# 7-product pairs of a hybrid decoder trunk: the block of the fourth sum's second half and its weights moved by 64 bytes, and four raw weight buffers for five

## The chip, the core and the metric

The kernel runs on one core of one Trainium2 chip. Its engines are TensorE (PE, whose weight loads the profile shows as PEld), VectorE (DVE), ScalarE (ACT), GpSimd (POOL) and SyncE (SP); each works through its own list of instructions, and semaphores order them among each other. The metric is the device time of one execution in microseconds.

## The reference, cut to what matters

Two layers work on x of 512 tokens and 1024 channels in float32. Each has a mixer sub-layer (four token mixers, gates and an output projection) and a gated feed-forward sub-layer. The change lies in the latter:

```python
hf = rms_norm(x, norm_ffn_pre[l])
u = causal_depthwise_conv(hf @ ffn_w_up[l], ffn_conv_w[l], ffn_conv_b[l])
gate, val = jnp.split(u, 2, axis=-1)
f = (jax.nn.gelu(gate, approximate=True) * val) @ ffn_w_down[l]
x = x + rms_norm(f, norm_ffn_post[l])
```

`ffn_w_up[l]` is 1024 x 5632: 22 blocks of 128 gate columns and 22 of value columns.

## The kernel before

**Arithmetic.** Each float32 operand is held as the sum of a high and a low part that PE takes (`hi`, `lo`). A product is three matmuls with 128x128 weights: high weights with the high and with the low activations, and low weights with the high activations. A weight unit comes by DMA from `wts` into a raw tile of 128x1024 (one of `NRAW` = 5, in `w_dma`), and is then split: ACT copies the high part into a tile `whi`, DVE subtracts to get `wlo`. There are four such pairs of tiles (`NSPL`). Each has 128 columns to spare, and `place` puts the units of the 7-product pairs (key `"fs"`) 16 columns, 64 bytes, further on in them.

**The up projection.** A pair i is one gate block and the value block that belongs to it. Pairs 0 and 1 run in the head of the stage (tile `hd`, 256-column matmuls), pairs 2 to 4 and 21 with 512-column matmuls (tile `ps`), and pairs 5 to 20 (`SEVEN`) with seven products of half size in place of eight: the 2x2 block form of a matrix product (two halves of the channels by two halves of the tokens) with sums of activations and sums of weights. In `seven(i)` a product is a call of `product(bank, weights, column, operand, first)`: 12 matmuls of 256 columns, for four blocks of 128 channels (kt) the triple high-high, high weights with low activations, low weights with high activations. Three PSUM banks, `sa`, `sb` and `se`, collect them. ACT copies (`ca`, `cb`) and DVE additions combine the parts, and `ffn_pair` makes from them the convolution, the gate and the product (`fu`).

A 7-product pair takes four weight units: 0 is the gate block from `wts`, 1 is sums of weights from a DRAM tensor that GpSimd's accumulating DMAs have made before, 2 is a half of such sums beside a half from `wts` (two DMAs into one raw tile), and 3 is a half more, which goes into a small slot (`rs`), not into a raw tile. Unit 2 is `w2`: its columns 0 to 511 meet the sum of activations `d3`, its columns 512 to 1023 the sum `d4`. The last two products of a pair (`four` and `three`) run between the first products of the next.

**The sums of activations.** `forms(h)` makes `d1` to `d4` on DVE before the 7-product pairs begin, for the first half of the four kt (h = 0) and for the second (h = 1). Each is then split by `hilo` into two of the `NG` = 60 small slots of 128x512: ACT the high part (`t1h` ... `t4h`), DVE the low part (`t1l` ... `t4l`). `side` hands the slices to `product`.

**Order.** SP and GpSimd run what the code emits, in that order; a raw tile's load is emitted in `w_dma` as soon as fewer than `NRAW` raw tiles are in use, and it waits on the chip until DVE has finished with the tile's former content. In the up projection PE too runs in the order of the code. ACT's and DVE's lists come from a scheduler that goes by the dependencies and its own estimates.

Of the kernel before, what the change touches and what calls it, by code (L numbers as in the profile page):

```python
# [10 lines left out]
F32R = mybir.dt.float32r  # L11
AF = mybir.ActivationFunctionType
ALU = mybir.AluOpType
# [19 lines left out]

WMAX = 1024

def place(k):


    return 16 if k[0] == "fs" else 0
# [12 lines left out]
NCST = 2120  # L52


NG = 60
NRAW = 5
NSPL = 4

MANUAL = {mybir.EngineType.SP, mybir.EngineType.Pool}
# [55 lines left out]
def build(tc, x, wts, prm, gains, cst, out, order=None):  # L115
# [3 lines left out]
    order = [] if recording else order  # L119
    V, A, G, T, SP = nc.vector, nc.scalar, nc.gpsimd, nc.tensor, nc.sync  # L120
    with ExitStack() as ctx:
        pool = lambda name, bufs, **k: ctx.enter_context(tc.tile_pool(name=name, bufs=bufs, **k))
        pc = pool("cst", 1)
# [8 lines left out]
        def nm(s):  # L132
            uid[0] += 1
            return f"{s}{uid[0]}"

        def slot(w=512, dt=F32, name="g"):
            return pg.tile([128, w], dt, tag="g", bufs=NG, name=nm(name))

# [6 lines left out]
        def f(t):  # L145
            return t.bitcast(F32)
# [11 lines left out]
        raw, parts = {}, {}  # L158
# [9 lines left out]
        def w_dma():  # L168
            while pos["dma"] < len(order) and sum(not isinstance(r, list) for r in raw.values()) < NRAW:
                i = pos["dma"]  # L170
# [65 lines left out]
        def split_tiles(i):  # L236
            ts = [pw.tile([128, WMAX + 128], F32R, tag=t, bufs=NSPL, name=nm(t)) for t in ("whi", "wlo")]
            return [t[:, place(order[i][1]):] for t in ts]

        def halves(i, *srcs):  # L240

            hi, lo = split_tiles(i)
            c = 0
            for s, n in srcs:
                A.activation(hi[:, c:c + n], s, AF.Copy)  # L245
                V.tensor_tensor(lo[:, c:c + n], s, f(hi[:, c:c + n]), op=ALU.subtract)  # L246
                c += n
            parts[i] = (hi, lo)

        def w_seven(i):  # L250

            r = raw.pop(i)
            halves(i, (r[0], 512) if isinstance(r, list) else (r, 1024))

        def w_split(q, roomy=False):
# [113 lines left out]
        def hilo(src, scale=1.0, name="hl"):  # L369
            dve(0.62)  # L370
            hi = slot(dt=F32R, name=name + "h")
            lo = slot(dt=F32R, name=name + "l")
            if scale == 1.0:
                A.activation(hi, src, AF.Copy)
                V.tensor_tensor(lo, src, f(hi), op=ALU.subtract)
            else:
                A.activation(hi, src, AF.Copy, scale=scale)
                V.scalar_tensor_tensor(lo, src, scale, f(hi), op0=ALU.mult, op1=ALU.subtract)
            return hi, lo
# [218 lines left out]
        pr = prm_tile()  # L598
        hT_hi = pc.tile([128, 8, 512], F32R, name="hT_hi")
        hT_lo = pc.tile([128, 8, 512], F32R, name="hT_lo")  # L600
        scr = {}
        for l in range(L):
            scr[l, 0] = pd.tile([S, D], F32, name=f"scr{l}a")
# [46 lines left out]
        for l in range(L):  # L650
# [59 lines left out]
            for kv, b in enumerate((kcb, vcb)):  # L710
                for g in range(2):
                    t = slot(name="F")
# [625 lines left out]
            for want in main_gen():  # L1338
                if isinstance(want, tuple):
                    while want[1] not in done:  # L1340
                        r = step()
# [8 lines left out]
                while (credit > 0 or behind() > MAXB) and state["alive"]:  # L1350
                    r = step()
# [45 lines left out]
            form = {n: [] for n in ("d1", "d2", "d3", "d4")}  # L1397

            def forms(h):
                def block(t, k, q):  # L1400
                    return f(t[:, k * 4 + h * 2:k * 4 + h * 2 + 2, q * 256:q * 256 + 256])
                hi, lo = (lambda k, q: block(hT_hi, k, q)), (lambda k, q: block(hT_lo, k, q))
                sub, add = ALU.subtract, ALU.add
                a, b = slot(name="ta"), slot(name="tb")
                V.tensor_tensor(v2(a), hi(0, 0), hi(0, 1), op=sub)
                V.tensor_tensor(v2(b), lo(0, 0), lo(0, 1), op=sub)
                V.tensor_tensor(a, a, b, op=add)
                form["d1"].append(hilo(a, name="t1"))
                V.scalar_tensor_tensor(v2(b), v2(a), -1.0, hi(1, 1), op0=ALU.mult, op1=sub)
                V.tensor_tensor(v2(b), v2(b), lo(1, 1), op=sub)  # L1410
                form["d2"].append(hilo(b, name="t2"))
                c = slot(name="tc")
                V.scalar_tensor_tensor(v2(c), v2(b), -1.0, hi(0, 0), op0=ALU.mult, op1=sub)
                V.tensor_tensor(v2(c), v2(c), lo(0, 0), op=sub)
                form["d3"].append(hilo(c, name="t3"))
                d = slot(name="td")
                V.scalar_tensor_tensor(v2(d), v2(b), -1.0, hi(1, 0), op0=ALU.mult, op1=sub)
                V.tensor_tensor(v2(d), v2(d), lo(1, 0), op=sub)
                form["d4"].append(hilo(d, name="t4"))

            def side(n, kt):
                if n in form:
# [4 lines left out]
            def product(b, w, c, n, first):  # L1427

                o = b[:, 0:256]
                kw = {} if first else {"skip_group_check": True}  # L1430
                for kt in range(4):
                    hi, lo = side(n, kt)
                    k = c + kt * 128
                    mm(o, wc(w[0], k), hi, first and kt == 0, False, **kw)
                    mm(o, wc(w[0], k), lo, False, False, **kw)
                    mm(o, wc(w[1], k), hi, False, kt == 3, **kw)
# [7 lines left out]
            def seven(i):  # L1444

                ba, bb, be = bank("sa"), bank("sb"), bank("se")
                sa, sb = slot(name="ca"), slot(name="cb")
                L_, R_ = slice(0, 256), slice(256, 512)  # L1450
                w0 = w_get(l, ("fs", i, 0))
                w_ahead(1)
                product(ba, w0, 0, (0, 0), True)
                A.activation(sa[:, L_], ba[:, L_], AF.Copy)
                w_ahead(2)
                more()
                product(bb, w0, 512, (1, 0), True)
                V.tensor_tensor(bb[:, L_], bb[:, L_], sa[:, L_], op=ALU.add)
                w1 = w_get(l, ("fs", i, 1))
                w_ahead(2)  # L1460
                product(ba, w1, 0, "d2", False)
                A.activation(sa[:, R_], ba[:, L_], AF.Copy)
                w_ahead()
                more()
                product(be, w1, 512, "d1", True)
                w2 = w_get(l, ("fs", i, 2))
                product(ba, w2, 0, "d3", False)
                A.activation(sb[:, L_], ba[:, L_], AF.Copy)
                w_ahead()

                def four():
                    product(ba, w2, 512, "d4", False)
                    V.tensor_tensor(ba[:, R_], be[:, L_], sb[:, L_], op=ALU.add)

                def three():
                    w3 = w_get(l, ("fs", i, 3))
                    product(be, w3, 0, (1, 1), False)
                    V.tensor_tensor(bb[:, R_], be[:, L_], sa[:, R_], op=ALU.add)
                    ffn_pair(i, [bb, ba], -1.0)
                rest.extend((four, three))  # L1480

            forms(0)
# [152 lines left out]
```

## Time and profile before

| | us |
|---|---|
| median of three runs | 1863.5 (1863.27 to 1864.52) |
| the profiled execution | 1876.15 |
| its span | 1874.3 |
| PE busy | 1851.3 (99%) |
| DVE busy | 1407.6 (75%) |
| ACT busy | 984.8 (53%) |
| granted TensorE clock, mean | 0.999 |

The profiled execution takes 12.65 us more than the median of the runs without a profile. A row of a timeline gives the start in microseconds from the span's start, the duration, the engine, the line, output and inputs by their names in the program, and in brackets the idle time before it with what ended it. A matmul's duration reaches past the start of the next, so the pace is read from start to start. "PEld" rows are the loads of weights into PE.

### The profile page before, as it was taken

To read this page: it belongs to the slowest core of one execution; us is meant where nothing else is said; L and a number is where in the kernel's file an instruction comes from. 1 tells how busy PE (TensorE), PEld (TensorE's weight loads), DVE (VectorE), ACT (ScalarE), POOL (GpSimd) and SP (SyncE) were. 2 spreads that over 40 slices of the span, in tenths; PEclk is the share of its full clock that TensorE was granted. 3 is DMA by queue.
4 is the path that set the end of the run, shared out by engine and by line. 5 is a ranking of instruction groups with operands and counts; after the bars stand their busy time and mean duration, and the time that the engine had idled before them with its cause. 6 is when DMAs were issued, how large, how long until landed. Compare 5 with 4: busy or idle time off the path is not lost.

```text
span 1874.3 us, 28621 instructions
## 1 busy us (share of the span) xinstructions
PE 1851.3 (99%) x10524; PEld 1622.7 (87%) x10524; DVE 1407.6 (75%) x2572; ACT 984.8 (53%) x1856; POOL 244.8 (13%) x397
## 2 busy tenths in 40 slices
PE   7999999999999999999999999999999999999998
PEld 7988888888788899988898888888878898999886
DVE  6898879888547888882468987897985578888732
ACT  5547576732435566662345675776224444666521
POOL 1403321100401000000023034201013010000000
PEclk9999999999999999999999999999999999999999
DMA  9524596765975356544465256958559653565332
GB/s 324 162 91 109 153 201 140 156 185 155 205 190 188 102 180 195 184 143 132 155 210 142 68 147 164 188 125 174 167 163 225 179 184 98 190 195 180 127 112 68
DMA packets 121069, 302.52 MB, mean 161 GB/s; under 512 B 16224, under 2 KB 16608, under 8 KB 120928
## 3 DMA queue, kind: packets, MB, share of 16 engines
q1 hardware_dynamic: 95328, 252.43, 42.4%
q0 software_dynamic: 25600, 48.26, 15.6%
q8 instruction: 83, 1.36, 0.3%
q14 instruction: 58, 0.48, 0.1%
HBM read 277.55 MB, written 75.50 MB: 188 GB/s over the span
## 4 chain that ended last, share of the span: by engine, by line
PE 95%; DVE 2%; issue 1%; ACT 1%; POOL 0%; DMA 0%; SPq 0%; DVEq 0%; POOLq 0%; ACTq 0%
PE ps L346 45%; PE tk L346 17%; PE sa L346 10%; PE hd L346 5%; PE se L346 5%; PE o L346 3%; PE sb L346 2%; PE vt L346 2%; PE sB L346 1%; PE sA L346 1%; PE tr L435 1%; PE tB L1128 1%; PE tA L1128 1%; PE cmp L346 0%; PE tA L1227 0%
## 5 line engine op out<-in xcount | busy, mean ns | idle before, releaser
L284 ACT ACTIVATE whi<-raw 128x1024 fp32r<-128x1024 f32 (+2 forms) x254 | 237.2, 940 | 450.8 <-PE ps L346 247.4
L285 DVE TENSOR_TENSOR wlo<-raw,whi 128x1024 fp32r<-128x1024 f32 (+2 forms) x254 | 271.0, 1072 | 211.8 <-ACT whi L284 210.2
L346 PE MATMUL ps<-hT_hi,whi 128*128 128x512 f32 x976 | 383.4, 393 | 0.9 <-DVE ob L1147 0.9
L346 PE MATMUL ps<-hT_hi,wlo 128*128 128x512 f32 x976 | 381.1, 390 | 0.0
L346 PE MATMUL ps<-hT_lo,whi 128*128 128x512 f32 x976 | 380.9, 390 | 0.0
L346 PEld LDWEIGHTS ps<-hT_hi,whi 128*128 128x128 f32 x976 | 183.4, 188 | 38.4 <-DVE ob L1147 1.7
L346 PEld LDWEIGHTS ps<-hT_hi,wlo 128*128 128x128 f32 x976 | 183.3, 188 | 38.3
L346 PEld LDWEIGHTS ps<-hT_lo,whi 128*128 128x128 f32 x976 | 183.5, 188 | 35.6
L950 DVE SCALAR_TENSOR_TENSOR acc<-ct,prm,acc 128x511 f32<-128x511 f32 (+14 forms) x240 | 175.5, 731 | 3.4
L246 DVE TENSOR_TENSOR wlo<-raw,whi 128x1024 fp32r<-128x1024 f32 x96 | 117.0, 1219 | 21.5 <-ACT whi L245 21.5
L346 PE MATMUL tk<-whi,fh 128*128 128x512 f32 x336 | 130.9, 390 | 0.0
L346 PE MATMUL tk<-whi,fl 128*128 128x512 f32 x336 | 130.8, 389 | 0.0
L346 PE MATMUL tk<-wlo,fh 128*128 128x512 f32 x336 | 130.7, 389 | 0.0
L401 POOL TENSOR_TENSOR sm<-sm,mhalf 128x1 f32<-128x1 f32 x32 | 22.1, 691 | 811.1 <-DVE sm L400 811.1
L245 ACT ACTIVATE whi<-raw 128x1024 fp32r<-128x1024 f32 x96 | 101.8, 1060 | 48.3 <-PE se L346 26.8
L1107 ACT ACTIVATE P<-P,sm 128x256 f32<-128x256 f32 (+3 forms) x128 | 70.6, 554 | 28.7 <-DVE sm L1105 28.3
L346 PEld LDWEIGHTS tk<-whi,fl 128*128 128x128 f32 x336 | 63.1, 188 | 13.2
L346 PEld LDWEIGHTS tk<-whi,fh 128*128 128x128 f32 x336 | 63.1, 188 | 13.0
L346 PEld LDWEIGHTS tk<-wlo,fh 128*128 128x128 f32 x336 | 63.1, 188 | 12.9
L346 PE MATMUL hd<-hT_hi,bh 128*128 128x256 f32 x256 | 64.5, 289 | 0.0
L346 PE MATMUL hd<-hT_hi,bl 128*128 128x256 f32 x256 | 63.6, 285 | 0.0
L214 POOL DMA_DIRECT2D sum<-wts x32 | 36.9, 1153 | 188.5 <-DMA sum<-wts 188.0
(354 smaller groups left out, 4731.0 us busy)
## 6 DMA issues: line engine op xcount, KB each, us to landing
raw<-wts SPq DMA_DIRECT2D x230, 512.0 KB, 4.2
raw<-wts SPq DMA_DIRECT2D x98, 256.0 KB, 4.3
sum<-wts SPq DMA_DIRECT2D x64, 256.0 KB, 5.0
sum<-wts SPq DMA_DIRECT2D x32, 512.0 KB, 5.8
sum<-wts POOLq DMA_DIRECT2D x64, 256.0 KB, 10.9
sum<-sum POOLq DMA_DIRECT2D x64, 256.0 KB, 11.1
raw<-sum SPq DMA_DIRECT2D x32, 512.0 KB, 4.1
br<-wts SPq DMA_DIRECT2D x40, 256.0 KB, 6.1
```

The source lines that it names most:

```text
L214: G.dma_start(s1, b(i + 1, 512), accum_op=ALU.add)
L245: A.activation(hi[:, c:c + n], s, AF.Copy)
L246: V.tensor_tensor(lo[:, c:c + n], s, f(hi[:, c:c + n]), op=ALU.subtract)
L284: A.activation(hi[:, c:c + n], s, AF.Copy)
L285: V.tensor_tensor(lo[:, c:c + n], s, f(hi[:, c:c + n]), op=ALU.subtract)
L346: T.matmul(o, lhsT=lhsT, rhs=rhs, start=start, stop=stop, **kw)
L401: G.tensor_tensor(v[:, 1:2], v[:, 0:1], mhalf[:, 0:1], op=ALU.pow)
L435: T.transpose(bs[t, h][:, k * 128:k * 128 + 128], y[h][:, k * 128:k * 128 + 128], ident)
L950: V.scalar_tensor_tensor(acc[i][:, k:], ct[i][:, :512 - k], w[:, 30 - k:31 - k], acc[i][:, k:], op0=ALU.mult, op1=ALU.add)
L1107: A.activation(P[i], P[i], AF.Exp, bias=mn[:, i:i + 1], scale=-1.0, accum_out=sm[:, i:i + 1])
L1128: T.transpose(B[j][:, (i - j) * 128:(i - j) * 128 + 128], P[i][:, j * 128:j * 128 + 128], ident)
```

## The change

Three things change.

- In unit 2 the second 512 columns lie 16 columns further on than before: the unit occupies 2 x 528 columns of its `whi` and `wlo` tile, of which 2 x 512 are written. The split writes both blocks with one ACT and one DVE instruction over a view of 128x2x512, and `four()` reads its weights from column `APART` = 528.
- For h = 1 the parts of `d4` go into a tile of their own, `t4`, at columns 16 to 527 (high) and 528 to 1039 (low), in place of two small slots. For h = 0 nothing changes.
- `NRAW` falls from 5 to 4 and `NG` from 60 to 59.

The number of instructions on each engine is the same as before. By the addresses that the built program gives the tiles, counted within 512 bytes, the activations of all sums and of `hT_hi` and `hT_lo` start at byte 416 and the weights of the 7-product units at byte 480, in both programs; in the changed one the moved weight block starts at byte 32, and the moved half of `d4` at byte 480.

```diff
+APART = 528
-NG = 60
-NRAW = 5
+NG = 59
+NRAW = 4
 ...
         def w_seven(i):
             r = raw.pop(i)
+            if order[i][1][2] == 2:
+                whole = split_tiles(i)
+                hi, lo = (t[:, :2 * APART].rearrange("p (k c) -> p k c", k=2)[:, :, :512] for t in whole)
+                v = r.rearrange("p (k c) -> p k c", k=2)
+                A.activation(hi, v, AF.Copy)
+                V.tensor_tensor(lo, v, f(hi), op=ALU.subtract)
+                parts[i] = tuple(whole)
+                return
             halves(i, (r[0], 512) if isinstance(r, list) else (r, 1024))
 ...
+        t4 = pc.tile([128, 1152], F32R, name="t4")
 ...
-                form["d4"].append(hilo(d, name="t4"))
+                if h == 0:
+                    form["d4"].append(hilo(d, name="t4"))
+                    return
+                hi_, lo_ = t4[:, 16:528], t4[:, 528:1040]
+                A.activation(hi_, d, AF.Copy)
+                V.tensor_tensor(lo_, d, f(hi_), op=ALU.subtract)
+                form["d4"].append((hi_, lo_))
 ...
                 def four():
-                    product(ba, w2, 512, "d4", False)
+                    product(ba, w2, APART, "d4", False)
```

The scheduler orders ACT and DVE anew. This is ACT in layer 0 where the 7-product pairs begin, before the change; `t3h` and `t4h` are high parts of the sums for h = 1, `fu` the first step of `ffn_pair` for pairs 3 and 4, `ca` the first copy of pair 5.

```order
L374 ACTIVATE t3h_6617<-tc_6614 128x512
L374 ACTIVATE t4h_6624<-td_6621 128x512
L1377 ACTIVATE fu_6693<-ps_6628,prm_75 128x512
L1377 ACTIVATE fu_6694<-ps_6659,prm_75 128x512
L1377 ACTIVATE fu_6765<-ps_6703,prm_75 128x512
L245 ACTIVATE whi_6806<-raw_6578 128x1024
L1377 ACTIVATE fu_6766<-ps_6734,prm_75 128x512
L1454 ACTIVATE ca_6778<-sa_6775 128x256
```

And ACT at the same place, changed:

```order
L387 ACTIVATE t3h_6616<-tc_6613 128x512
L1392 ACTIVATE fu_6687<-ps_6625,prm_75 128x512
L1392 ACTIVATE fu_6688<-ps_6656,prm_75 128x512
L1392 ACTIVATE fu_6762<-ps_6697,prm_75 128x512
L249 ACTIVATE whi_6803<-raw_6645 128x1024
L1392 ACTIVATE fu_6763<-ps_6731,prm_75 128x512
L1438 ACTIVATE t_78<-td_6620 128x512
L1475 ACTIVATE ca_6775<-sa_6772 128x256
```

The high part of the fourth sum (`t4h`, now `t`) has moved behind four `fu` and a `whi`, directly ahead of `ca`.

DVE there before the change, from the last step of the fourth sum, `td`, on:

```order
L1418 TENSOR_TENSOR td_6621<-td_6621,hT_lo 128x512
L375 TENSOR_TENSOR t4l_6625<-td_6621,t4h_6624 128x512
L1380 SCALAR_TENSOR_TENSOR fu_6693<-ps_6628,prm_75,fu_6693 128x511
L1380 SCALAR_TENSOR_TENSOR fu_6694<-ps_6659,prm_75,fu_6694 128x511
L1380 SCALAR_TENSOR_TENSOR fu_6693<-ps_6628,prm_75,fu_6693 128x510
L1380 SCALAR_TENSOR_TENSOR fu_6765<-ps_6703,prm_75,fu_6765 128x511
L1380 SCALAR_TENSOR_TENSOR fu_6694<-ps_6659,prm_75,fu_6694 128x510
L246 TENSOR_TENSOR wlo_6807<-raw_6578,whi_6806 128x1024
L1380 SCALAR_TENSOR_TENSOR fu_6765<-ps_6703,prm_75,fu_6765 128x510
L1380 SCALAR_TENSOR_TENSOR fu_6766<-ps_6734,prm_75,fu_6766 128x511
```

And changed:

```order
L1395 SCALAR_TENSOR_TENSOR fu_6687<-ps_6625,prm_75,fu_6687 128x511
L1395 SCALAR_TENSOR_TENSOR fu_6688<-ps_6656,prm_75,fu_6688 128x511
L1433 TENSOR_TENSOR td_6620<-td_6620,hT_lo 128x512
L1395 SCALAR_TENSOR_TENSOR fu_6762<-ps_6697,prm_75,fu_6762 128x511
L1395 SCALAR_TENSOR_TENSOR fu_6687<-ps_6625,prm_75,fu_6687 128x510
L1395 SCALAR_TENSOR_TENSOR fu_6688<-ps_6656,prm_75,fu_6688 128x510
L1395 SCALAR_TENSOR_TENSOR fu_6762<-ps_6697,prm_75,fu_6762 128x510
L250 TENSOR_TENSOR wlo_6804<-raw_6645,whi_6803 128x1024
L1395 SCALAR_TENSOR_TENSOR fu_6763<-ps_6731,prm_75,fu_6763 128x511
L1439 TENSOR_TENSOR t_78<-td_6620,t_78 128x512
L1479 TENSOR_TENSOR sb_6773<-sb_6773,ca_6775 128x256
```

The low part of the fourth sum (`t4l`, now `t`, L1439) has moved behind the `fu` and the first `wlo`, and the last step of `td` behind two `fu`.

## Rows read from the trace of the kernel before

**Rows 1.** The page: busy time, share and count of each engine over the span.

```profile
PE 1851.3 (99%) x10524; PEld 1622.7 (87%) x10524; DVE 1407.6 (75%) x2572; ACT 984.8 (53%) x1856; POOL 244.8 (13%) x397
```

**Rows 2.** PE's waits: engine, tile, line, releaser; total us, times, longest.

```profile
PE sa L346 <- ACT ca L1454: 0.8, 2, 0.4
```

**Rows 3.** Windows, head then 7-product: us; busy PE, PEld, DVE, ACT, POOL; PEclk, DMA, GB/s.

```profile
606.30:615.90 9.60, 9.60 (x82) 9.60 (x82) 6.49 (x8) 5.61 (x7) 0.00 (x0) 1.00 0.67 220
700.00:790.00 90.00, 90.00 (x767) 90.00 (x766) 77.35 (x111) 62.01 (x92) 0.00 (x0) 1.00 0.60 188
```

**Rows 4.** Tiles `hd`, then `sa`, weight loads: ns least/median/most, first and last start.

```profile
L346 PEld LDWEIGHTS hd<-hT_lo,bh x256: 192/192/192, 15.8 to 1544.7; 128*128 128x128 f32 x128
...
L346 PEld LDWEIGHTS sa<-t4h,whi x128: 187/192/193, 659.2 to 1737.5; 128*128 128x128 f32 x128
L346 PEld LDWEIGHTS sa<-t4l,whi x128: 187/188/192, 659.4 to 1737.6; 128*128 128x128 f32 x128
```

**Rows 5.** PE's timeline: start, us, engine, line, operation [idle before, releaser].

```profile
640.22 0.39 PE L346 MATMUL ps<-hT_lo,whi 128*128 128x512 f32 x1
...
642.03 0.39 PE L346 MATMUL ps<-hT_hi,whi 128*128 128x512 f32 x1
...
652.90 0.28 PE L346 MATMUL sb<-hT_hi,wlo 128*128 128x256 f32 x1
653.58 0.39 PE L346 MATMUL sa<-t2h,whi 128*128 128x256 f32 x1 [0.40 <-ACT ca L1454]
653.81 0.29 PE L346 MATMUL sa<-t2l,whi 128*128 128x256 f32 x1
```

**Rows 6.** ACT's timeline at the start of layer 0's 7-product stretch.

```profile
649.01 0.63 ACT L374 ACTIVATE t4h<-td 128x512 fp32r<-128x512 f32 x1 [2.70 <-DVE td L1418]
649.55 2.10 ACT L1377 ACTIVATE fu<-ps,prm 128x512 f32<-128x512 f32 x3
651.53 1.06 ACT L245 ACTIVATE whi<-raw 128x1024 fp32r<-128x1024 f32 x1
652.48 0.78 ACT L1377 ACTIVATE fu<-ps,prm 128x512 f32<-128x512 f32 x1
653.14 0.39 ACT L1454 ACTIVATE ca<-sa 128x256 f32<-128x256 f32 x1
```

**Rows 7.** DVE's timeline there.

```profile
649.67 0.69 DVE L375 TENSOR_TENSOR t4l<-td,t4h 128x512 fp32r<-128x512 f32 x1 [0.70 <-ACT t4h L374]
650.34 3.39 DVE L1380 SCALAR_TENSOR_TENSOR fu<-ps,prm,fu 128x511 f32<-128x511 f32 x5
```

**Rows 8.** SP's DMA issues in the steady 7-product stretch.

```profile
742.37 0.33 SPq L182 DMA_DIRECT2D raw<-sum  x1
...
744.20 0.43 SPq L185 DMA_DIRECT2D raw<-wts  x1
746.63 0.33 SPq L188 DMA_DIRECT2D raw<-wts  x1
752.26 0.33 SPq L182 DMA_DIRECT2D raw<-sum  x1
```

**Rows 9.** ACT's timeline there: splits of the raw tiles loaded by Rows 8.

```profile
754.17 1.06 ACT L245 ACTIVATE whi<-raw 128x1024 fp32r<-128x1024 f32 x1 [0.96 <-PE se L346]
...
761.19 1.06 ACT L245 ACTIVATE whi<-raw 128x1024 fp32r<-128x1024 f32 x1 [0.35 <-PE sb L346]
```

**Rows 10.** The page, DMA issues: count, KB each, median us from issue to landing.

```profile
raw<-wts SPq DMA_DIRECT2D x230, 512.0 KB, 4.2
```

**Rows 11.** End of layer 0's mixer: DMA issues, SP's and ACT's timeline.

```profile
raw<-wts SPq DMA_DIRECT2D x3, 512.0 KB, 11.0
...
497.27 5.35 SPq L188 DMA_DIRECT2D raw<-wts  x4
...
508.95 0.63 ACT L284 ACTIVATE whi<-raw 128x512 fp32r<-128x512 f32 x1 [0.72 <-ACT th L927]
```

**Rows 12.** ACT's timeline in layer 0's down projection.

```profile
896.94 0.63 ACT L275 ACTIVATE bh<-raw 128x512 fp32r<-128x512 f32 x1 [4.83 <-DMA raw<-wts]
```

## The prediction

> **What bounds the kernel now.** I read the page first: TensorE is busy for 99% of the span [rows 1]. The reader is to see there that only two things can move the time: a change in the pace at which matmuls follow each other, or a stall of PE made or removed. Next come PE's waits: the one wait that lies in the stretch that the change touches is that of `sa` for ACT's `ca`, 0.8 us in two places, one for each layer [rows 2]. Third, the windows: in the 7-product stretch PE and the weight load are both busy for the whole 90 us, DVE for 77.35 us and ACT for 62.01 us, at a granted clock of 1.00 [rows 3]. So there a weight load of 128x128 runs under every matmul of 256 columns and never stops; where both are full, the pace is set by how soon load and matmul let each other go on.
>
> That pace differs by place. The windows count every record that touches them, and a matmul of 0.28 us touches the next two, so some 2.4 records are to be taken off: 9.60/(82-2.4) = 120.6 ns in the head's 256-column matmuls, 90.00/(767-2.4) = 117.7 ns in the 7-product stretch [rows 3]. The loads agree: 192 ns in the head's last group; in a 7-product group 192 ns for the first of each three, but 188 ns for the next [rows 4]. In the built program before, the head's weight blocks start at the same byte as its moving operand, counted within 512 bytes; those of the 7-product units lie 64 bytes further. So a distance of 64 bytes goes with about 120.6 - 117.7 = 2.9 ns less for each matmul.
>
> **Placement, part by part.** The 7-product stretches hold 32 pairs of 84 matmuls, 2,688 in all. The change moves the second block of each third weight unit, and the half of the fourth sum that it calls `t4`. Matmul counts and instruction shapes stay, so only the distance between a running matmul's moving operand and the block loaded under it changes. From the addresses of the two built programs: 160 transitions have both operands moved, distance still 64 bytes, cost 0; 30 lose it (the last matmul on `t4` against the next product's unmoved weights), 30 x 2.9 ns = +0.09 us; 222 go to 128 bytes (the two k-tiles of the fourth sum that stay in place, and the transitions into them). The trace of before has no stretch at 128 bytes. From above, 128 acts as 0 does: 222 x 2.9 = +0.6 us. From below, the load ceases to pace at all: 512-column matmuls, whose loads hide, follow each other in (642.03 - 640.22)/8 = 0.226 us [rows 5], 113 ns for 256 columns, so 222 x (113.1 - 117.7) = -1.0 us. I take 0, the value at 64 bytes, the nearest row in distance. The rest of the 2,688 stay as they are.
>
> The Trainium skill, "SBUF — State Buffer", section "Who interferes with whom", states that PE reads SBUF through two independent ports, one for the moving operand and one for the weight load, and that PE never waits on anyone. By that rule no address could matter, the placement term would be 0 and the sum 1862.15 instead of the 1862.2 below. The 188 and 192 ns [rows 4] speak against it, though weakly, since head and 7-product groups differ in more than addresses.
>
> **The split in one operation over two blocks.** ACT and DVE each write 2x512 instead of 1024 elements, 32 times each. The nearest rows: on ACT 0.95 us from start to start for 1,024 elements (651.53 to 652.48) and 0.54 us for 512 (649.01 to 649.55) [rows 6]. Were the two halves paid as two instructions, that would be 0.13 us more for each pair, on an engine with idle time in every pair. Below nothing there is no reason for a gain. Taken at 0 either way for the end: ACT has 28 us idle in 90, DVE 12.65 [rows 3].
>
> **ACT's order at the start of the 7-product stretch.** This is the largest term. PE's matmul of 652.90 is followed by one at 653.58 instead of 653.02, and the next comes 0.23 us later instead of 0.12 [rows 5]: 0.56 + 0.11 = 0.67 us lost, in layer 1 likewise (the second of the two waits [rows 2]); together 1.34 us. What PE waits for is ACT: `t4h` sits 2.70 us on DVE's `td` until 649.01, and three `fu`, a `whi`, a `fu` and then `ca` queue behind it, so `ca` starts at 653.14 and ends at 653.53 [rows 6]. In the changed order that activation stands behind these five, directly ahead of `ca`. The three `fu` then run in what was ACT's wait for `td` (their sums are finished by 645 us, since a 24-matmul chain of 226 ns takes 5.4 us and the last one ends at about 650.2). The `whi` needs the split tile that this last chain frees, so it starts at about 650.2; 650.2 + 0.95 + 0.66 + 0.54 gives `ca` a start at about 652.35 and an end at 652.74. PE would be due at 653.02. So the stall goes whole, with 0.28 us to spare less the signal from ACT to PE (0.05 us in before, 653.53 to 653.58): -0.67 us x 2 = -1.34 us. Bounds: 0 if another wait puts `ca` back by 0.8 us or more, and not more than -1.34, because behind it PE is at its pace. What is late next: DVE computes the low part of `t4` at 649.67, after 0.70 us of waiting; in the new order seven `fu` of 0.66 us and a `wlo` of some 1.1 us go ahead of it, and the wait is gone: 649.67 - 0.70 + 5.8 = 654.8 [rows 7]. The first load for the fourth product starts at 659.2 [rows 4], and six matmuls on its first half take 0.7 us more before that part is read. 4.4 us remain.
>
> **Four raw buffers.** Each load now waits for one release more, so it is issued when the load behind it was. In the steady 7-product stretch SP issues one pair's three loads at 742.37, 744.20 and 746.63, and the next pair's first at 752.26 [rows 8]; the splits that read the first and the third start at 754.17 and 761.19 [rows 9]. A load takes 4.2 us [rows 10]. Shifted by one, these two land at 748.4 and 756.5: 5.8 and 4.7 us ahead of their splits. Cost 0; the cover is those 4.7 us. At the end of the mixer it is thinner: four loads are issued from 497.27 on, some 1.7 us apart, and take 11.0 us at the median, so the first lands by about 508.3 for a split at 508.95 [rows 11]. Shifted by 1.7 us it would come about 1 us late for ACT; PE, which has no wait for a load or a split in its list, reads such a tile later still. In the down projection ACT already waits for a load, 4.83 us at 896.94 [rows 12], and PE, which reads those tiles only in the next stage, has no wait of that kind. I take 0 for all three, with up to +1 us for the range from the mixer's end. The 60th small slot is given up together with two slots that the fourth sum no longer takes, so nothing waits longer for a slot in the stretch.
>
> **Sum.** Against the profiled execution: span 1874.3 + 0.09 - 1.34 = 1873.0, execution 1876.15 - 1.25 = 1874.9. The runs' median, 1863.5, lies 12.65 us (0.7%) below that execution; a term of 1.25 us is the same in both: 1863.5 - 1.25 = 1862.2 us.
>
> **Rivals.**
> - The stall stays, or another takes its place: `ca` still comes late since the `fu` or the `whi` ahead of it wait for something that the row does not show. For it: in before ACT ran those five back to back, so their own waits are hidden. Against: their producers' rows end by 650.2. Time: 1863.5 + 0.09 = 1863.6.
> - The distance of 128 bytes has a price of its own: 1862.8 if it acts as 0 does, 1861.2 if loads are freed. Nothing in the trace speaks for either.
> - The change does not do what it says: a 64-byte step has no effect on any transition, and the 2.9 ns of the head come from something else. Then -1.34 alone: 1862.15. The skill's rule on ports above is this case.
> - Slower: four buffers starve the splits of the 7-product stretch. It decides where a load takes more than 4.2 + 4.7 = 8.9 us. Were they as slow as at the mixer's end, 11.0 us [rows 11], each pair's third split would be 2.1 us late, and if PE had no distance to it, 32 x 2.1 = +67 us: 1929. Against it: 4.2 us there, in a stretch whose DMA share is 0.60 [rows 3].
>
> **How the numbers follow.** Forecast 0.51 (1862.2). No address effect at all 0.10 (1862.15). Stall stays 0.19 (1863.6). A price of 128 bytes 0.12 (1861.2 to 1862.8). Starved splits, in full or in part, 0.05, ending above 1867.2. On the fast side 0.03 is left for what no row shows: 3.7 us over the 222 transitions would be 17 ns each, three times the bound. About 0.2%, or 3.7 us, is what a measurement of this kernel can tell from no change; every case but the last two lies within it: faster 0.03, same 0.92, slower 0.05. The range: low 1863.5 - 1.34 - 1.04 = 1861.1, less 0.2 for the runs' own lower spread, 1860.9; high 1863.6 + 0.6 + 1.0 for late loads = 1865.2. These leave out some 0.1 to 0.15.
>
> **What would show it.** Right: no gap of 0.68 us ahead of the first `sa<-t2h` of each layer, the wait of `sa` for `ca` gone from PE's list, the pace there 117.7 ns still, load times of 188 and 192 in the fourth product as elsewhere. Wrong: a new entry in PE's waits on `whi` or `wlo` or on raw loads, ACT waiting for a load in the 7-product stretch, a pace of the fourth product under 115 or at 120 ns, or a span that moved by more than 3 us.

## The result: 15 us slower, of which the first profiles show 4.5

| | us |
|---|---|
| before, median (4 runs beside the changed kernel) | 1863.38 (1863.12 to 1864.52) |
| changed, median of 4 runs | 1878.62 (1877.27 to 1880.66) |
| ratio, with its 95% interval | 1.0081 (1.0064 to 1.0099) |
| changed, profiled execution and its span | 1880.66, 1878.9 |
| before, the execution behind the rows above, and its span | 1876.15, 1874.3 |

The forecast was 1862.2 us, within 0.2% of before. The profiled execution of the changed kernel is one of its four runs, the longest; that of before lies 12.65 us over the median of its own. So the two profiles differ by 4.5 us where the runs differ by 15.2, and whoever compares the two traces alone looks for the wrong thing.

What the prediction looked at first went as it said. Changed kernel, the page's busy times:

```profile
PE 1852.7 (99%) x10524; PEld 1624.5 (86%) x10524; DVE 1408.0 (75%) x2572; ACT 986.8 (53%) x1856; POOL 244.0 (13%) x397
```

PE is busy for 99% as in [rows 1], 1.4 us more in all, and that tells nothing of what follows. PE's waits (engine, tile, line, releaser; total us, times, longest):

```profile
PE sA L359 <- DVE mix L945: 1.5, 2, 0.8
PE ps L359 <- DVE ob L1162: 1.4, 2, 0.7
PE sC L359 <- DVE pcTl L388: 1.0, 2, 0.5
PE sB L359 <- DVE sm L1120: 1.0, 2, 0.5
```

The wait of `sa` for `ca` [rows 2] is gone; the waits of `sA` and `sB` are new, that of `ps` for `ob` and of `sC` are longer than in the kernel before:

```profile
PE ps L346 <- DVE ob L1147: 0.9, 2, 0.4
PE sC L346 <- DVE pcTl L375: 0.7, 2, 0.4
```

ACT's timeline at the start of layer 0's 7-product stretch in the changed kernel, to be read beside [rows 6]:

```profile
648.38 2.10 ACT L1392 ACTIVATE fu<-ps,prm 128x512 f32<-128x512 f32 x3
652.34 1.06 ACT L249 ACTIVATE whi<-raw 128x1024 fp32r<-128x1024 f32 x1 [1.85 <-PE ps L359]
653.30 0.76 ACT L1392 ACTIVATE fu<-ps,prm 128x512 f32<-128x512 f32 x1
653.97 0.62 ACT L1438 ACTIVATE t<-td 128x512 fp32r<-128x512 f32 x1
654.48 0.37 ACT L1475 ACTIVATE ca<-sa 128x256 f32<-128x256 f32 x1
```

The stretch begins at 652.36 here, so `ca` starts 2.12 us into it (the working had 2.16) and PE goes on without a gap, where [rows 5] had 0.68 us. PE's timeline, changed kernel:

```profile
655.07 0.28 PE L359 MATMUL sb<-hT_hi,wlo 128*128 128x256 f32 x1
655.19 0.28 PE L359 MATMUL sa<-t2h,whi 128*128 128x256 f32 x1
```

That gap was more than a loss: in most executions of the kernel before, PE goes over to a faster pace behind it, as the following runs show.

### The profile page after: what moved, and what is told of

Same layout as the page of the kernel before. It is cut to its first block, busy times and chain, and to the rows that moved or that the text cites. A ratio compares the mean times of both kernels' runs of the same rounds, so it can differ in the third digit from the quotient of the medians.

```text
span 1878.9 us, 28672 instructions
## 1 busy us (share of the span) xinstructions
PE 1852.7 (99%) x10524; PEld 1624.5 (86%) x10524; DVE 1408.0 (75%) x2572; ACT 986.8 (53%) x1856; POOL 244.0 (13%) x397
## 3 DMA queue, kind: packets, MB, share of 16 engines
q8 instruction: 82, 1.34, 0.3%
## 4 chain that ended last, share of the span: by engine, by line
PE 96%; DVE 2%; issue 1%; POOL 0%; ACT 0%; DMA 0%; SPq 0%; DVEq 0%; POOLq 0%; ACTq 0%
PE ps L359 45%; PE tk L359 17%; PE sa L359 10%; PE hd L359 5%; PE se L359 5%; PE o L359 3%; PE sb L359 2%; PE vt L359 2%; PE sB L359 1%; PE sA L359 1%; PE tr L448 1%; PE tB L1143 1%; PE tA L1143 1%; PE cmp L359 1%; DVE wlo L298 0%
## 5 line engine op out<-in xcount | busy, mean ns | idle before, releaser
L249 ACT ACTIVATE whi<-raw 128x1024 fp32r<-128x1024 f32 x64 | 67.9, 1061 | 43.1 <-PE se L359 26.8
L250 DVE TENSOR_TENSOR wlo<-raw,whi 128x1024 fp32r<-128x1024 f32 x64 | 78.1, 1220 | 16.4 <-ACT whi L249 16.4
```

## The experiments

The pace of the stretch is read as in the prediction, from a window of 90 us: 90.00/(x - 2.4), with x the count of matmuls. Paces of single products and gaps between starts are read from PE's timeline, from one matmul's start to the next. "Wait" below is PE's wait for `ca` at the third product of pair 5.

### The two kernels again

No edit.

> The kernel before, unchanged, timed and profiled anew. In the result the changed kernel took 1878.6 us and this one 1863.4 us, 15.2 us apart, but the two profiled executions lie only 4.5 us apart (1880.66 and 1876.15). Theory A (the profiled execution of before was itself not like its timed ones, by 12.7 us of pace): a new profile lies near 1863 to 1866 us, and its rows show where those 12.7 us were. Theory B (a profile costs this kernel 12.7 us, and costs the changed one less): the new profile again lies near 1876 us and the rounds near 1863.5 us.

> The changed kernel, unchanged, on the same chip as the one before. If the 15 us belong to the kernel: 1877 to 1881 us, ratio 1.0075 to 1.009. If they belong to the chip or the moment of the first measurement: 1866 to 1869 us, the 4.5 us that the two first profiles show.

Before: 1864.43 us, profile 1864.46, so theory A holds. Changed: 1878.33 us. The windows of before profiled anew, and of the changed kernel's first profile (us; busy PE, PEld, DVE, ACT, POOL with counts; PEclk, DMA share, GB/s):

```profile
700.00:790.00 90.00, 90.00 (x797) 90.00 (x796) 80.91 (x113) 62.52 (x95) 0.00 (x0) 1.00 0.62 194
```

```profile
700.00:790.00 90.00, 90.00 (x765) 90.00 (x764) 77.41 (x111) 61.34 (x91) 0.00 (x0) 1.00 0.60 187
```

That is 113.3 and 118.0 ns a matmul; [rows 3], from the odd execution of before, had 117.7. So the stretch has **two paces**, at the same granted clock (1.00), with the same instructions. Over the whole stretches the means are 113.6 and 118.0 ns: 2,686 steps x 4.4 ns = 11.8 us; 0.6 us of it is the price of the moved operands, as a run below shows. The odd profile of before accounts for itself: 117.86 - 113.59 = 4.27 ns, 11.5 us of the 11.7 between its span and the new one (1862.6).

Where the pace changes is plain in PE's timeline of before anew; the rows are the first matmul of each product of 12, layer 0:

```profile
649.88 0.28 PE L346 MATMUL sa<-hT_hi,whi 128*128 128x256 f32 x1
...
651.29 0.28 PE L346 MATMUL sb<-hT_hi,whi 128*128 128x256 f32 x1
...
653.28 0.39 PE L346 MATMUL sa<-t2h,whi 128*128 128x256 f32 x1 [0.41 <-ACT ca L1454]
...
654.78 0.28 PE L346 MATMUL se<-t1h,whi 128*128 128x256 f32 x1
...
656.14 0.28 PE L346 MATMUL sa<-t3h,whi 128*128 128x256 f32 x1
...
657.50 0.28 PE L346 MATMUL sa<-hT_hi,whi 128*128 128x256 f32 x1
```

Ahead of the wait 1.41 us for a product (12 x 117.8 ns), behind it 1.36 us (12 x 113.3), to the end of the stretch. The 89 executions of before that were timed beside the other kernels of this study fall into three groups: 63 at 1862.9 to 1865.3 us, 21 at 1869.3 to 1871.2 and 5 at 1875.1 to 1876.0. They lie 6 us apart, half of 11.8: both layers at the faster pace, one, or none. For the first and the third group there is a trace; that the middle one is one layer of each is inferred. How often the faster pace is missed differs from chip to chip: in 1 of 26 executions on one, in 12 of 16 on another. Why is open.

### Buffers alone, moved weights alone

```diff
-NG = 60
-NRAW = 5
+NG = 59
+NRAW = 4
```

> The kernel before with 4 raw buffers and 59 small slots, and no operand moved. Theory 'buffers' (the later loads and the order that follows from them cost the time): 1877 to 1880 us, all of the loss. Theory 'placement' (the 64 and 128 byte distances cost it): 1862 to 1868 us, at most the 4.5 us of waits that the two profiles show in the mixers.

1868.69 us (1866.11 to 1870.96), ratio 1.0023 (1.0013 to 1.0032). The wait is in place, and the stretch ran at the faster pace in both layers; the loss lies outside it, in the mixers. Layer 0's window:

```profile
700.00:790.00 90.00, 90.00 (x796) 90.00 (x796) 81.76 (x115) 62.77 (x95) 0.00 (x0) 1.00 0.61 192
```

The next run is the kernel before with the changed split and the fourth product's weights from column 528, `t4` in its slots:

```diff
-                    product(ba, w2, 512, "d4", False)
+                    product(ba, w2, APART, "d4", False)
```

> The kernel before (5 raw buffers, 60 slots) in which only the weight block of the fourth product moves by 64 bytes, while the whole fourth sum stays in its slots: so all 384 matmuls of the fourth product run at a distance of 128 bytes instead of 222. Theory 'placement': 12 us or more above before, since more transitions lie at 128 bytes than in the changed kernel (1875 to 1885 us). Theory 'buffers': 1862 to 1864 us, no loss.

1865.76 us, ratio 1.0007 (0.9997 to 1.0016). The fourth product took 118.1 ns a matmul, everything else 113.3 to 113.4. So 128 bytes cost 4.8 ns at the faster pace, about 1.8 us over 384 matmuls, and do not by themselves end that pace. Neither half by itself explains 15 us.

### The changed order without moved operands

```diff
-APART = 528
+APART = 512
 ...
-                hi_, lo_ = t4[:, 16:528], t4[:, 528:1040]
+                hi_, lo_ = t4[:, 0:512], t4[:, 512:1024]
```

> The changed kernel with its 4 raw buffers, 59 slots, its own tile t4 and its order of instructions on every engine, but with every operand where the kernel before has it: the fourth product's weights at column 512, t4 from column 0 on. Every transition of the 7-product stretch is at 64 bytes again. Theory 'stall' (what the change lost is the short wait of PE for ca, after which the kernel before runs at 113.4 ns a matmul instead of 117.8): no wait, 117.8 ns throughout, 1876 to 1880 us, as slow as the changed kernel. Theory 'placement' (the distances of 0 and 128 bytes hold the pace down): 113.4 ns and 1866 to 1869 us.

1878.05 us, as slow as the changed kernel, with every transition at its old 64 bytes: 90/(766 - 2.4) = 117.9 ns in both layers, and no wait in the stretch.

```profile
700.00:790.00 90.00, 90.00 (x766) 90.00 (x766) 77.37 (x110) 62.16 (x92) 0.00 (x0) 1.00 0.60 187
```

So the pace is lost without any moved operand. The kernel of the run with 4 raw buffers and 59 slots differs from this one in the order of ACT and DVE, in the split over two blocks and in `t4` as a tile of its own; it has the wait and the faster pace, and this one has neither. That it is the wait is what the next runs test.

The means of the two stretches also give the price of the moved operands at the slower pace: 118.01 - 117.78 = 0.23 ns over 2,686 steps, 0.6 us.

### The wait put back

```diff
-                A.activation(sa[:, L_], ba[:, L_], AF.Copy)
+                for _ in range({5: 2}.get(i, 1)):
+                    A.activation(sa[:, L_], ba[:, L_], AF.Copy)
```

> The changed kernel, in which the first copy (ca) of the first 7-product pair of each layer is made twice, so that PE waits for it again by some 0.5 to 0.8 us; nothing else. Theory 'stall': after that wait 113.4 ns in all products but the fourth, whose 222 transitions at 128 bytes stay at 118 to 120 ns: 1878.3 - 11.9 + 1.9 for the fourth product + 1.3 for two waits = about 1870 us. Theory 'placement': 117.8 to 118 ns stay, and the added wait comes on top: 1879 to 1880 us.

1880.2 us: by the time alone the wait changes nothing, but the trace shows what happened. PE's timeline, first matmul of each product:

```profile
656.42 0.38 PE L359 MATMUL sa<-t2h,whi 128*128 128x256 f32 x1 [0.35 <-ACT ca L1476]
...
657.90 0.28 PE L359 MATMUL se<-t1h,whi 128*128 128x256 f32 x1
...
659.26 0.28 PE L359 MATMUL sa<-t3h,whi 128*128 128x256 f32 x1
...
660.62 0.28 PE L359 MATMUL sa<-hT_hi,whi 128*128 128x256 f32 x1
...
661.99 0.28 PE L359 MATMUL sa<-t4h,whi 128*128 128x256 f32 x1
...
663.40 0.28 PE L359 MATMUL sb<-hT_hi,whi 128*128 128x256 f32 x1
...
664.82 0.28 PE L359 MATMUL sa<-t2h,whi 128*128 128x256 f32 x1
```

Behind the wait the products take 1.36 us, until the first fourth product (`t4h`); from there on 1.41 us to the end. The faster pace begins at the wait, and it ends at the fourth product in its changed places. The expectation "stall" held for three products.

The same in the middle, with `{13: 4}` in place of `{5: 2}`:

> The changed kernel, in which the first copy of pair 13, the ninth of 16, is made four times in each layer, so that PE waits some 1 to 1.5 us in the middle of the stretch. Theory 'stall': 117.8 ns up to pair 13 and 113.4 ns from there on (the fourth product apart), so half of the gain for the same wait: 1878.3 - 5 + 2.5 = about 1876 us, and the step in the pace stands at pair 13 in both layers. If the pace is set at the start of the stretch or by the kind of execution, no step: 1880 to 1881 us.

1880.09 us, the time of the second case; the trace shows the step of the first. PE's timeline around pair 13:

```profile
733.14 0.38 PE L359 MATMUL sa<-t2h,whi 128*128 128x256 f32 x1 [0.20 <-ACT ca L1476]
...
734.61 0.28 PE L359 MATMUL se<-hT_hi,whi 128*128 128x256 f32 x1
...
735.97 0.28 PE L359 MATMUL se<-t1h,whi 128*128 128x256 f32 x1
...
740.06 0.28 PE L359 MATMUL sa<-t4h,whi 128*128 128x256 f32 x1
...
741.47 0.28 PE L359 MATMUL sb<-hT_hi,whi 128*128 128x256 f32 x1
```

1.36 us from the wait to the fourth product (734.61 to 740.06 in four products), 1.41 us after it; layer 1 does the same. So a wait in the middle of the stretch starts the faster pace too.

With the wait and the operands at their old places (the edit above joined to that of the run without moved operands):

> The changed kernel with the first copy of pair 5 made twice and with every operand at its old place (all of the stretch at 64 bytes): 4 raw buffers, 59 slots, tile t4, but the wait of PE is back. Theory 'wait and address' (a wait moves PE from 117.8 to 113.4 ns; the 30 transitions at 0 bytes or the 222 at 128 move it back): 113.4 ns in both layers to their ends where the wait takes, 1866 to 1870 us. If the wait's effect always dies at the first fourth product, whatever the addresses: 1879 to 1881 us.

Of its profiled execution (1875.77 us) layer 0 ran at 113.4 ns to the end, past all its fourth products, and layer 1 at 117.8, its wait without effect:

```profile
700.00:790.00 90.00, 90.00 (x796) 90.00 (x795) 81.76 (x115) 62.52 (x94) 0.00 (x0) 1.00 0.60 191
1620.00:1710.00 90.00, 90.00 (x767) 90.00 (x766) 77.60 (x110) 61.42 (x91) 0.00 (x0) 1.00 0.58 185
```

The other three runs took 1878.18 to 1881.87 us; by these times the wait mostly failed in them, of which there is no trace. So a wait can start the faster pace and does not do so every time. Over all profiled layers of this study with such a wait (0.48 to 0.69 us from start to start) and 64 bytes behind it, 15 changed pace and 5 did not. The interval behind the wait goes with the outcome: from the first matmul to the next it is 227 ns in all 5 that stayed at 117.8, and 221 to 223 ns in the 15. It is no rule: with 229 ns behind a shorter wait (the last run of "Which part of the fourth product ends the faster pace") the pace changed all the same. What decides is not known.

### Distances

The kernel before, with another column for the 7-product weights (in `place`):

```diff
-    return 16 if k[0] == "fs" else 0
+    return 0
```

and 64 in place of 16:

> The kernel before with the 7-product units' weights at column 0 instead of 16, so that all transitions of the stretch are at a distance of 0 bytes, as in the head; the wait for ca stays. If a wait alone sets the fast pace, 113.4 ns and 1864 us. If it needs a distance of 64 bytes as well: the head's 120 ns, 2,688 x 6.5 ns = +17 us, about 1881 us.

> The kernel before with the 7-product units' weights at column 64 instead of 16, a distance of 256 bytes for the whole stretch; the wait for ca stays. Open: 0 bytes gave 120.0 ns with and without a wait, 64 bytes 117.8 before a wait and 113.4 behind one, 128 bytes 117 to 120. If the pace has a floor at 113.4 that a large distance reaches by itself, the first two products, ahead of the wait, run at 113.4 too: 1863 to 1865 us in every execution. If it behaves as 128 bytes: 117 to 119 ns, 1875 to 1878 us.

1881.41 us and 1882.09 us. Each layer of both has its wait and stays at 120.0 ns: 90/(752 - 2.4) in the first, at 0 bytes.

```profile
700.00:790.00 90.00, 90.00 (x752) 90.00 (x751) 75.93 (x108) 60.97 (x89) 0.00 (x0) 1.00 0.59 183
```

A whole stretch at 0 or at 256 bytes showed no faster pace; of the distances that a whole stretch was run at, only 64 bytes has it. The Trainium skill ("SBUF — State Buffer", "Who interferes with whom") gives PE two independent SBUF read ports, one for the moving operand and one for the weight load. The trace does not agree with the reading that addresses therefore cost nothing: the distance alone moves the pace from 117.8 to 120.0 ns. By what path, no run here shows.

### Which part of the fourth product ends the faster pace

Both runs have the second copy in pair 5. In the first only the weights lie apart (`t4` from column 0), in the second only `t4` (`APART = 512`):

> As the run before, and the fourth product's weights alone at column 528: 382 transitions at 128 bytes, none at 0 behind t4. If the distance of 0 behind t4 ends the fast pace: 113.4 ns stays between the fourth products, these run at some 118 ns, 1868 to 1872 us. If 128 bytes ends it: 117.8 ns from the first fourth product on, 1879 to 1881 us.

> As the last but one, and the second half of the fourth sum alone moved by 64 bytes, its weights not: 190 transitions at 0 bytes, none at 128. If the distance of 0 ends the fast pace: 113.4 ns up to the first fourth product, then 117.8 ns, 1879 to 1882 us. If it is 128 bytes that ends it: 113.4 ns elsewhere and 120 ns in these 190: 1867 to 1871 us.

1870.68 and 1870.35 us; the second time lies in the range of one of its cases, but neither case describes what happened. With the weights apart and 382 transitions at 128 bytes the faster pace stays between the fourth products, which take 118.1 ns. With `t4` apart the wait had no effect in either layer (227 ns behind it), and the first fourth product itself set the faster pace. PE's timeline, first matmul of each product:

```profile
658.13 0.28 PE L359 MATMUL sa<-t3h,whi 128*128 128x256 f32 x1
...
659.55 0.28 PE L359 MATMUL sa<-hT_hi,whi 128*128 128x256 f32 x1
...
660.96 0.28 PE L359 MATMUL sa<-t4h,whi 128*128 128x256 f32 x1
...
662.38 0.28 PE L359 MATMUL sb<-hT_hi,whi 128*128 128x256 f32 x1
...
663.76 0.28 PE L359 MATMUL sa<-t2h,whi 128*128 128x256 f32 x1
```

A product takes 1.41 or 1.42 us up to 662.38, then 1.38, and 1.36 from there on, but for the later fourth products and those behind them. So 128 bytes alone do not end the faster pace, and `t4` alone starts it. To see the latter without any wait, the changed kernel with `APART = 512` and nothing else:

> The changed kernel without the moved weight block: only the second half of the fourth sum lies 64 bytes further on, so 190 transitions are at 0 bytes and none at 128; no wait is added. If transitions at 0 bytes among those at 64 move PE into the faster pace: 117.8 ns up to the first fourth product of each layer, then 113.4 ns (about 115 in the fourth products), 1867 to 1870 us. If only a wait does that: 117.8 ns throughout, 1878 to 1880 us.

1869.11 us: 117.8 ns up to the first fourth product of each layer, 113.4 behind it, 115.1 in the fourth products and 114.5 in the product after each. Undoing the moved weight block alone, then, takes back some 9.5 us of the loss (1878.6 - 1869.1, from two chips).

Two runs asked if 0 bytes as such do it, in the kernel without moved operands: pair 5's weights of the fourth product at column 624 (0 bytes for 12 matmuls), and only its last two k-tiles there (6 matmuls). In these edits a pair of numbers is the first column of the weights and what is added from the third k-tile on:

```diff
+    return (624, 0) if i == 5 else (512, 0)
```

```diff
+    return (512, 112) if i == 5 else (512, 0)
```

> The changed kernel with every operand at its old place (1878 us, 117.8 ns throughout), except that in pair 5, the first 7-product pair of each layer, the weights of the fourth product lie at column 624, so that its 12 matmuls are at 0 bytes; split in three pieces. If 0 bytes in one product is enough: 113.4 ns from the product behind it on, 1866 to 1869 us. If not: 1877 to 1880 us.

> As the run before, but only the last two k-tiles of pair 5's fourth product are at 0 bytes (6 matmuls), as where t4 alone was moved. If it is the step from 64 to 0 and back to 64 bytes that moves the pace: 113.4 ns behind it, 1866 to 1869 us. If the state persists: 1877 to 1880 us.

1877.65 and 1879.79 us, 117.8 ns throughout but 120.0 and 118.7 ns in those products. A step to 0 bytes by the weights' address in one pair is not enough; with `t4` the moving operand's address steps too, which may be what counts but was not tested by itself. The last of these runs has `t4` apart, and of the weights only the half that meets it: 16 columns are added from the third k-tile on, and the second copy of pair 5 is there:

```diff
+    return (512, 16)
```

> The changed kernel with the first copy of pair 5 made twice (PE's wait), and of the fourth product's weights only the half that meets t4 moved by 64 bytes: 160 transitions with both operands moved at 64 bytes, 30 at 0 behind them, 32 at 128 into them, where the changed kernel has 222. If the 128 bytes end the faster pace there: 113.4 ns stays in all products, 1867 to 1870 us. If those with both operands moved end it: 117.8 ns from the first fourth product on, 1879 to 1881 us.

1869.28 us, 113.4 ns and 115.5 in the fourth products. Here the wait left only 0.25 us between two starts, 0.13 more than without one, and the faster pace began right behind it in both layers, ahead of the first fourth product. The transitions with both operands moved and the last one at 0 bytes do not end the faster pace, then, nor do 32 transitions at 128. Each part of the changed fourth product keeps the faster pace; only the two together, as the changed kernel has them, ended it, in both profiled runs with a wait. Why is open.

### Where the buffers' 4 us are, and a kernel without either fault

> The kernel before with 59 small slots instead of 60 and nothing else. If the slots cost what the run with 4 raw buffers and 59 slots lost (through PE's order in the mixers, which differs from before with 59 slots and hardly with 4 raw buffers): 1867 to 1871 us, PE waits of 0.5 to 0.8 us at sA, sB and sC in both layers. If it is the raw buffers: 1863 to 1866 us.

The edit is `NG = 59` alone: 1869.42 us (1866.21 to 1870.81), with both layers at the faster pace in the profile. Beside it on that chip before had a median of 1864.8, ratio 1.0010 (0.9997 to 1.0022), but 10 of its 23 executions belong to the second group; against the first group's 1864 it is some 5 us. So the slot costs what both counts together cost, and the raw buffer next to nothing. Its PE waits, where before has none at `sA` and `sB`:

```profile
PE sA L346 <- DVE mix L930: 1.6, 2, 0.8
PE ps L346 <- DVE ob L1147: 1.4, 2, 0.7
PE sB L346 <- DVE sm L1105: 1.0, 2, 0.5
```

These are 3.1 us more than in the list of before; that of `sC` (0.7 us) did not grow here, against the expectation. The rest comes behind them. Window of the same run, columns as above:

```profile
293.80:297.20 3.40, 3.40 (x11) 2.63 (x10) 3.40 (x13) 2.50 (x9) 0.00 (x0) 0.56 0.53 166
```

The granted clock is 0.56 on average there, so for most of the window it is at the lower of its two levels (1.2 GHz), and seven or eight 512-column matmuls follow each other in 426 ns instead of 227: 1.5 us, in none, one or both layers of an execution (none in the changed kernel's second profile, one in its first, two here). The clock of the 12 runs goes with their times: 0.997 on average in the six of 1869.6 to 1870.8 us, 0.998 at 1868.3 and 1869.3, 0.999 in the four of 1866.2 to 1867.7. So most of this kernel's spread goes with these drops.

The last kernel is the changed one with these edits:

```diff
-NG = 59
+NG = 60
-APART = 528
+APART = 512
 ...
-        t4 = pc.tile([128, 1152], F32R, name="t4")
+        t4 = pc.tile([128, 1024], F32R, name="t4")
 ...
-                hi_, lo_ = t4[:, 16:528], t4[:, 528:1040]
+                hi_, lo_ = t4[:, 0:512], t4[:, 512:1024]
```

The tile now stands ahead of `hT_hi`, so that all fits; there its first column lies 64 bytes further on than the other sums, as column 16 did. `NRAW` stays at 4:

> The changed kernel without the moved weights and with 60 small slots; the second half of the fourth sum still lies 64 bytes further on (its tile is 1024 columns and stands ahead of hT_hi, so that it fits). If the 59 slots cost the mixers' 4 us and the move of t4 sets the faster pace by itself: no wait for ca, 117.8 ns up to the first fourth product, then 113.4 ns, with some 115 in the fourth products: 1864.4 - 1.3 + 1.5 + 0.9 = about 1865 us in all executions, with none at 1870 or 1876 as the kernel before has. If the raw buffers cost the 4 us: 1868 to 1870 us.

1864.89 us in 12 runs from 1864.18 to 1865.55, against 1864.8 (1862.86 to 1871.21) for 23 of before on that chip, 10 of them over 1869; ratio 0.9987 (0.9976 to 0.9998). Window:

```profile
700.00:790.00 90.00, 90.00 (x793) 90.00 (x793) 80.32 (x113) 62.56 (x95) 0.00 (x0) 1.00 0.64 196
```

and PE's waits; for `sA`, `sB` and `sa` there is none, and of the others named above there are these:

```profile
PE sC L359 <- DVE pcTl L388: 1.0, 2, 0.5
PE ps L359 <- DVE ob L1162: 0.9, 2, 0.4
```

The faster pace, 90/(793 - 2.4) = 113.8 ns with its fourth products, comes without a wait for `ca`, and the mixers have before's waits, but for 0.3 us more at `sC`, as in the run with 4 raw buffers and 59 slots. The median is that of before; what the kernel gains is that all 12 runs lie within 1.4 us, which points to both layers at the faster pace every time.

## Why the prediction was wrong, step by step

The step that failed is the assumption that PE runs at one pace on both sides of the wait, so that taking the wait out could only gain; the runs show two paces, and 11.8 us between them.

- **The pace that bounds the stretch.** Read as one figure, 117.7 ns, from a single execution [rows 3, 5]. It was the slower of two, and that execution was of a kind that makes 5 of 89. The step shows in the sum: "lies 12.65 us (0.7%) below that execution" was written down and then taken as a constant, though the same text held two figures that would have pointed to it: 117.7 ns and the 113.1 ns of a hidden load, 4.6 ns x 2,688 = 12.4 us.
- **The wait.** That it goes, and when `ca` would start, was right (to 0.04 us); the low part of `t4` came 4.31 us into the stretch where the working had 4.6. The step "not more than -1.34, because behind it PE is at its pace" was wrong: the term was not -1.34 but -1.3 + 11.2, about +10 us, for in most executions the wait put PE at its faster pace (11.2 is 11.8 less the 0.6 of the moved operands). The bounds excluded a loss on the ground of the very assumption at fault, and no rival let the wait's absence cost anything.
- **Placement.** 222 transitions at 128 bytes were put at 0 (-1.0 to +0.6 us). At the pace that the changed kernel has, they cost 0.6 us with the 30 at 0 bytes, about the upper bound. That in their changed places the fourth products also end the faster pace, so that the wait put back did not help, was not thought of. The split in one operation over two blocks takes 1.06 us on ACT and 1.22 us on DVE, as over one block: 0, as taken.
- **The rival "no address effect".** The distance does matter, 0 and 256 bytes against 64 by 2.2 ns at least.
- **Four raw buffers.** Put at 0 with up to +1 us; the run with 60 slots and 4 raw buffers agrees. The working expected ACT about 1 us late for a load at the mixer's end; it waited 5.13 us at 510.04 and 4.63 us at 1439.56. Its waits for loads into `bh`, most of them in the down projection, grew from 11.8 to 14.1 us in all. No wait of PE came of either, and ACT waits for no load in the window of the 7-product stretch: the starvation rival did not occur.
- **The 60th slot.** No wait of PE in the stretch came of it, as said, but it was looked at nowhere else: in the mixers it cost 3.1 us of waits and up to 3 us at the lower clock. The prediction has no term for it.

The sum as the runs give it: +11.8 for the pace (0.6 of it the moved operands), -1.3 for the waits, +4.6 for the slot (3.1 of waits and, as in the changed kernel's first profile, 1.5 in one layer at the lower clock), about 15.1 us, of 15.2 measured (13.9 in the second measurement).

## What to carry to other kernels

If the profiled execution is slower than the runs by more than its like, find the stretch where it is so before costing anything: divide the difference by the count of the commonest instruction. In this kernel, where load and matmul of PE are both busy all the time, the pace was not a property of the code alone, and a short wait could set it; so a plan to remove a wait needs the pace on both sides of it, from more than one execution. And a buffer given up for a change in one stage is to be followed through every stage that draws on the same pool.

## What the runs showed of the hardware that was not expected

- 256-column matmuls with a weight load under each ran at 113.4 or at 117.8 ns at the same granted clock, and each pace held for over 150 us where nothing moved it. At the faster pace (before, profiled anew) every load took 187 or 188 ns; at the slower the first of each three took 192 ns and the other two 187 or 188.
- A wait that left 0.48 to 0.69 us between two starts was followed by the faster pace in 15 of 20 layers, with 221 to 223 ns from the first matmul to the next, and not in 5, with 227 ns. In the run with `t4` and half the weights apart 0.25 us at the wait, with 229 ns behind it, was enough in both layers.
- With `t4` alone 64 bytes further on, the first fourth product started the faster pace in all 6 layers of three kernels, without an effective wait.
- 0 and 256 bytes between the moving operand and the next weights, for the whole stretch, gave 120.0 ns with no second pace, and 192 ns for every load; 128 bytes in the fourth products gave 118.1 ns there, with 113.4 around them.
- Two waits of PE in the mixers, of 0.75 and 0.70 us, the second ending 1.43 us behind the first, were followed in some executions, and not in others, by seven or eight 512-column matmuls at the lower clock (0.56 on average from 293.80 to 297.20 us).
